# adaLN weights of a two-layer trunk in uncut 2 MB units with a buffer of their own

## The chip, the cores and the metric

The kernel runs on one core of one Trainium2 chip. The metric is device time in microseconds of one execution, the median of several. A core has five engines with queues of their own: TensorE (PE), VectorE (DVE), ScalarE (ACT), GpSimd (POOL) and SyncE (SP), and DMA engines that they share; here SP issues the weight loads.

## The reference

One inference step of a trunk of two layers for 256 latent and 128 context tokens, width 1024, fp32. Every layer is modulated by adaLN: nine vectors of 1024 (shift, scale and gate, three times) come from a product of the SiLU of a conditioning vector with a weight matrix of 1024 x 9216. There are two conditioning vectors, one for latent tokens and one for context tokens, so the product has two rows, but it reads all 36 MB of each layer's matrix.

```python
def adaln(cvec, l, p):
    m = jax.nn.silu(cvec) @ p['w_ada'][l] + p['b_ada'][l]
    return m.reshape(cvec.shape[0], N_MOD, D_MODEL)

def trunk_layer(x, mod, l, p, pos, ctx):
    sh1, sc1, g1, sh2, sc2, g2, sh3, sc3, g3 = [mod[:, i, None, :] for i in range(N_MOD)]
    x = x + 0.5 * g1 * swiglu(modulate(rms_norm(x, nw[0]), sh1, sc1), ...)
    m, new_ctx = mixer(modulate(rms_norm(x, nw[1]), sh2, sc2), l, p, pos, ctx)
    x = x + g2 * m
    x = x + 0.5 * g3 * swiglu(modulate(rms_norm(x, nw[2]), sh3, sc3), ...)
```

The mixer has one input projection and three heads beside each other (differential attention, latent attention `mla`, and a two-way S5 scan), then one output projection. Shift and scale of a part are needed before it begins, its gate when its first output rows are added to x.

## The kernel before

Activations stay on the chip, transposed (128 partitions of features x 8 blocks x 384 tokens). The program is, per layer, ffn(l, 0), mixer(l), ffn(l, 1). Every big product is made of three matmuls on split operands (`mm3`, lines 238 to 241): ACT copies a weight tile into `whi`, VectorE or POOL subtracts to get `wlo` (`split`, line 249), each with two buffers. Weight tiles come through `load` (line 243): 1 MB, [128, 2048], three buffers under one tag `raw`, issued on SP in program order. An up block of an ffn is 48 matmuls of a tile, a down block 36 or 30. The first 2048 adaLN columns of layer 0 are done ahead of everything with loads of their own (`start`, lines 1412 to 1426); all others are the subject here.

The remaining adaLN columns are cut into groups (`ada_steps`, line 278). Groups 0, 1 and 3 of a layer have 2048 columns, in 8 units of one k row (128 of the 1024 rows of the matrix); the other groups have 1024 columns, in 4 units of two k rows. A unit is one 1 MB `load` from the common ring and four matmuls per k row (line 293): the stationary operand is `conds`, 32 columns with two in use, and each of the four matmuls writes a quarter of the partitions of one PSUM bank, `adaps`, so that a k row of a group is four matmuls of 512 or 256 columns. In fp32 a matmul shows as two records in the profile: a k row has 8. At a group's end ACT copies the bank (`ad`), TensorE transposes it (line 301) and VectorE adds the bias in four instructions.

The units are steps in a list, `fillers`; the stages pop them at fixed places. An ffn pops one step after each up and each down block (`fill_after`), the mixer one after each of the products 3, 4 and 5 of its input projection, the rest spread evenly over 36 attention steps, and the last beside the output projection. Before, ffn(0, 0) has 12 units, mixer 0 has 32, both middle ffns have 2 each, and mixer 1 has 16. The steps of the preparation of the S5 tables (`prep`) sit in the same list in both ffns ahead of a mixer. One of them, `kext`, writes a table to DRAM (`kd`, line 752) and reads it back as 2048 pieces of 512 B (`Wi`, line 756), both on POOL's queue. A scheduler then places instructions on every engine; a matmul may be placed among others than those it is written beside. PE runs its own list strictly in order, and so does SP.

Of the kernel before, what the change touches and what calls it, by code (L numbers as in the profile page):

```python
# [20 lines left out]
DEPTH = 2  # L21
# [44 lines left out]
def _layout(inp):  # L66
    a = {k: np.asarray(v) for k, v in inp.items()}
    d = {}
# [3 lines left out]
    wa = w[:, :, :8192].reshape(2, 8, 128, 4, 2048).transpose(0, 3, 1, 2, 4).reshape(2, 32, 128, 2048)  # L72
    wb = w[:, :, 8192:].reshape(2, 4, 2, 128, 1024).transpose(0, 1, 3, 2, 4).reshape(2, 4, 128, 2048)
    d['wada'] = np.concatenate([wa, wb], 1)
    for z in range(2):
        wc = w[:, :, 4096 + 1024 * z:5120 + 1024 * z].reshape(2, 4, 2, 128, 1024).transpose(0, 1, 3, 2, 4)
        d['wada'][:, 16 + 4 * z:20 + 4 * z] = wc.reshape(2, 4, 128, 2048)
    d['wada'][0, :8] = w[0, :, :2048].reshape(8, 128, 2, 8, 128).transpose(3, 1, 0, 2, 4).reshape(8, 128, 2048)
# [98 lines left out]
def trunk(ctx, tc, I, O):  # L177
# [8 lines left out]
    def bank(name):  # L186
        return psp.tile([128, 512], F32, tag="P", name=name)
# [5 lines left out]
    def SMV(n):  # L193
        return sm[:, SM[n][0]:SM[n][1]]
# [38 lines left out]
    def act(out, a, f, **k):  # L233
        S.activation(out, a, f, **k)  # L234
# [40 lines left out]
    adaT = [cst.tile([128, 72, 2], F32, name=f"adaT{l}") for l in range(DEPTH)]  # L275
    bada = SMV('b_ada').rearrange("p (l b) -> p l b", l=2)

    def ada_steps(l, g):
        w = 512 if g in (0, 1, 3) else 256
        units = w // 64  # L280
        row = int(8 * g)
        st = {}

        def unit(u):
            raw = load(I['wada'][l, row + u])
            if u == 0:
                st['ps'] = psp.tile([128, 512], F32, tag="ada", name="adaps", bufs=1)
            ps = st['ps']
# [6 lines left out]
            if u == units - 1:  # L295
                ad = sp.tile([128, 512], F32, tag="ad", name="ad")
                act(ad[:, :w], ps[:, :w], AF.Copy)
                pt = bank("adapt")
                nch = w // 128
                for c in range(nch):  # L300
                    T.transpose(pt[:, c * 128:(c + 1) * 128], ad[:, c * 128:(c + 1) * 128], ident)
                b0 = 2 * row
                pv = pt[:, 0:nch * 128].rearrange("p (c q x) -> p q c x", c=nch, q=4)[:, :, :, 0:2]
                ov = adaT[l][:, b0:b0 + 4 * nch, :].rearrange("p (q c) x -> p q c x", c=nch)
                bv = bada[:, l, b0:b0 + 4 * nch].rearrange("p (q c) -> p q c", c=nch)
                for q in range(4):
                    add(ov[:, q], pv[:, q], bv[:, q, :, None].broadcast_to([128, nch, 2]))

        return [lambda u=u: unit(u) for u in range(units)]
# [336 lines left out]
    def s5_prep(l, s5p):  # L646
# [85 lines left out]
        def kext():  # L732
# [19 lines left out]
            nc.gpsimd.dma_start(kd.rearrange("c h g n -> g c h n"), kx.rearrange("p h j c -> p h (j c)"))  # L752
# [3 lines left out]
            nc.gpsimd.dma_start(wi.rearrange("p h g n -> p (h g) n"), win)  # L756
            P['Wi'] = wi

# [35 lines left out]
        steps += [lambda d=d, hf=hf: gtab(d, hf) for d in range(2) for hf in range(4)]  # L794
# [603 lines left out]
    def start(stp):  # L1398
# [4 lines left out]
        bv = bada[:, 0, 0:16].rearrange("p (z k) -> p z k", z=2)  # L1403
        pss = [[bank("up"), bank("up")] for _ in range(NF)]
        nx = 0
        for k in range(NB):
# [4 lines left out]
            raw = stp.tile([128, 2048], F32, tag="araw", name="araw", bufs=4)  # L1411
            nc.sync.dma_start(raw, I['wada'][0, k])
# [50 lines left out]
    N1, N2 = 16, 18  # L1463
    
    for l in range(DEPTH):
# [48 lines left out]
_NAMES = ('xT', 'wada', 'wfi', 'wfo', 'win', 'wout', 'wsm', 's5', 'small', 'lam', 'kc', 'vc', 'ckvc', 'kpec', 'const')  # L1514
# [14 lines left out]
```

## Time and profile before

| what | us |
|---|---|
| median of 3 runs | 1699.22 (1698.43 to 1699.89) |
| profiled execution, its own time | 1697.89 |
| its span | 1695.6 |
| PE busy | 1640.5 (97%) |
| VectorE busy | 1098.6 (65%) |
| ACT busy | 689.2 (41%) |
| POOL busy | 157.3 (9%) |
| mean granted clock of TensorE | 0.99 of full speed |

The span is the time between the first and the last instruction of the profiled execution. Busy time is an average over stages that differ, so the stages are read by themselves below: ffn(0, 0) from 46.0 us to 338.1, the products of mixer 0's input projection to 411.5, its attention and output projection to 586.4, ffn(0, 1) and ffn(1, 0) to 1163.1, the same two parts of mixer 1 to 1236.5 and 1399.7, and ffn(1, 1) to the end. A duration in the trace is that of one instruction or of a run of alike ones; consecutive matmuls overlap, so that the distance of two starts is less than the duration of one.

### The profile page before, as it was taken

The numbers are of one execution on the slowest core, as the hardware profiler recorded it, in microseconds if no ns is written. First come the engines' busy times: TensorE is split into PE (matmuls) and PEld (weight loads), VectorE is DVE, ScalarE is ACT, GpSimd is POOL, SyncE is SP. The second block draws the span as 40 slices with busy tenths as digits, with TensorE's granted clock in tenths as the row PEclk, the third lists the DMA queues.
The fourth block names the chain that finished last, engine by engine and source line by source line (L and its number), as shares of the span: only waits on it lengthen the run. The fifth ranks groups of instructions, "written<-read, shape, count | busy, mean of one in ns | idle before, by whom it ended". The sixth has DMA issues, their size and how long they took to land.

```text
span 1695.6 us, 26141 instructions
## 1 busy us (share of the span) xinstructions
PE 1640.5 (97%) x10144; PEld 1494.0 (88%) x10144; DVE 1098.6 (65%) x2752; ACT 689.2 (41%) x1295; POOL 157.3 (9%) x220
## 2 busy tenths in 40 slices
PE   7999999999999999999999999999998899999997
PEld 6888999998555899999999999999974589999997
DVE  6974576757465887577666555557745766555555
ACT  4332333533454533343344333335235654333333
POOL 1210110023001400000000000001301040000000
PEclk9999999999999999999999999999998999999999
DMA  9554542444576443354353333435436033333432
GB/s 377 198 214 163 140 151 97 157 162 144 191 270 237 139 171 118 125 124 137 93 180 137 118 136 109 141 95 172 148 128 226 26 103 122 125 124 112 139 101 84
DMA packets 45931, 251.47 MB, mean 148 GB/s; under 512 B 5600, under 2 KB 10576, under 8 KB 23920
## 3 DMA queue, kind: packets, MB, share of 16 engines
q1 hardware_dynamic: 41360, 241.12, 41.3%
q0 software_dynamic: 2144, 4.54, 1.1%
q10 hardware_dynamic: 2304, 4.15, 0.8%
q8 instruction: 79, 1.29, 0.3%
q14 instruction: 44, 0.36, 0.1%
HBM read 246.73 MB, written 3.05 MB: 147 GB/s over the span
## 4 chain that ended last, share of the span: by engine, by line
PE 88%; DVE 6%; ACT 3%; issue 1%; DMA 1%; POOL 0%; SPq 0%; DVEq 0%; ACTq 0%; POOLq 0%
PE up L239 15%; PE up L241 14%; PE up L240 14%; PE down L239 7%; PE down L241 7%; PE down L240 7%; PE adaps L293 4%; PE pj L239 2%; PE pj L241 2%; PE pj L240 2%; PE pout L241 1%; PE pout L239 1%; PE pout L240 1%; PE sc L1210 1%; PE po L1172 1%
## 5 line engine op out<-in xcount | busy, mean ns | idle before, releaser
L234 ACT ACTIVATE whi<-raw 128x1024 fp32r<-128x1024 f32 (+3 forms) x360 | 332.5, 925 | 660.0 <-PE up L240 337.1
L239 PE MATMUL up<-hh,whi 128*128 128x386 f32 x1408 | 474.4, 342 | 7.7 <-ACT whi L234 4.0
L241 PE MATMUL up<-hh,wlo 128*128 128x386 f32 x1408 | 478.3, 340 | 0.5 <-DVE wlo L213 0.5
L240 PE MATMUL up<-hl,whi 128*128 128x386 f32 x1408 | 478.3, 340 | 0.0
L213 DVE TENSOR_TENSOR wlo<-raw,whi 128x1024 fp32r<-128x1024 f32 (+2 forms) x318 | 347.5, 1093 | 49.0 <-ACT whi L234 46.2
L239 PEld LDWEIGHTS up<-hh,whi 128*128 128x128 f32 x1408 | 266.2, 190 | 15.5 <-ACT whi L234 5.3
L241 PEld LDWEIGHTS up<-hh,wlo 128*128 128x128 f32 x1408 | 265.6, 189 | 9.0 <-DVE wlo L213 2.2
L240 PEld LDWEIGHTS up<-hl,whi 128*128 128x128 f32 x1408 | 266.1, 189 | 1.5 <-issue 1.1
L241 PE MATMUL down<-hidh,wlo 128*128 128x384 f32 x704 | 236.3, 336 | 0.0
L239 PE MATMUL down<-hidh,whi 128*128 128x384 f32 x704 | 235.8, 335 | 0.0
L240 PE MATMUL down<-hidl,whi 128*128 128x384 f32 x704 | 235.3, 334 | 0.0
L231 DVE SCALAR_TENSOR_TENSOR xTt<-down,gate,xTt 128x256 f32<-128x256 f32 (+1 forms) x256 | 95.0, 413 | 115.0 <-PE down L241 115.0
L466 DVE COPY bb<-up 128x2 f32<-128x2 f32 x176 | 27.6, 158 | 190.3 <-PE up L241 189.8
L241 PEld LDWEIGHTS down<-hidh,wlo 128*128 128x128 f32 x704 | 132.1, 188 | 1.1 <-issue 0.6
L239 PEld LDWEIGHTS down<-hidh,whi 128*128 128x128 f32 x704 | 132.2, 188 | 1.0 <-ACT whi L234 0.8
L240 PEld LDWEIGHTS down<-hidl,whi 128*128 128x128 f32 x704 | 132.2, 188 | 0.0
L213 DVE TENSOR_TENSOR t<-up,R 128x384 f32<-128x384 f32 x176 | 95.5, 548 | 3.3 <-ACT R L234 3.2
L293 PE MATMUL adaps<-raw,conds 128*32 128x256 f32 (+1 forms) x704 | 85.3, 505 | 1.2 <-DMA raw<-in_wada 1.2
L239 PE MATMUL pj<-hh,whi 128*128 128x386 f32 (+1 forms) x240 | 84.3, 353 | 0.9 <-ACT whi L234 0.7
L234 ACT ACTIVATE hidh<-sl 128x384 fp32r<-128x384 f32 x88 | 46.1, 524 | 91.1 <-DVE sl L231 91.1
L241 PE MATMUL pj<-hh,wlo 128*128 128x386 f32 (+1 forms) x240 | 83.0, 347 | 0.0
L240 PE MATMUL pj<-hl,whi 128*128 128x386 f32 (+1 forms) x240 | 82.7, 346 | 0.0
(268 smaller groups left out, 1955.6 us busy)
## 6 DMA issues: line engine op xcount, KB each, us to landing
raw<-in_wfi SPq DMA_DIRECT2D x85, 1024.0 KB, 4.9
raw<-in_wada SPq DMA_DIRECT2D x64, 1024.0 KB, 5.1
raw<-in_wfo SPq DMA_DIRECT2D x32, 768.0 KB, 4.3
raw<-in_wfo SPq DMA_DIRECT2D x32, 640.0 KB, 4.0
raw<-in_win SPq DMA_DIRECT2D x14, 1024.0 KB, 4.8
araw<-in_wada SPq DMA_DIRECT2D x8, 1024.0 KB, 9.8
raw<-in_wout SPq DMA_DIRECT2D x16, 512.0 KB, 3.4
wr<-in_wfi SPq DMA_DIRECT2D x8, 384.0 KB, 9.7
```

The source lines that it names most:

```text
L213: return (eng or V).tensor_tensor(out, a, b, op=op)
L231: return V.scalar_tensor_tensor(out, a, s, b, op0=op0, op1=op1)
L234: S.activation(out, a, f, **k)
L239: T.matmul(out, whi, xhi, start=first, stop=False)
L240: T.matmul(out, whi, xlo, start=False, stop=False)
L241: marks.append(T.matmul(out, wlo, xhi, start=False, stop=last).ins)
L293: T.matmul(ps[32 * q:32 * q + 32, 0:w], conds[:, k, :], raw[:, c0:c0 + w], start=(k == 0), stop=(k == 7))
L466: V.tensor_copy(bb[:, z], ps[z][:, NT:NT + 2])
L1172: T.matmul(po[64 * h2:64 * h2 + 64, 0:256], vt[:, kt, 128 * b + 64 * h2:128 * b + 64 * h2 + 64], wTs[h2][:, kt, :], start=(kt == 0), stop= ...
L1210: T.matmul(sc, qT[p, self.b, t * 128:(t + 1) * 128], kT[p, self.b, self.k0:self.k0 + n], start=True, stop=True)
```

## The change

The columns of both layers behind the first 2048 are laid side by side and cut into eight groups of 2048 columns, each of 4 units of two k rows: a unit is one 2 MB load and eight matmuls of 512 columns. The units have a buffer of their own (`araw`, 16 KB per partition, one buffer) instead of the ring's. A unit's step is followed in the list by a step that issues the next unit's load, placed on SP behind the latest ring load written before it. A unit's matmuls may not be scheduled ahead of the latest `mm3` written before them (`issue_after(marks[-1])`). Groups 0 and 1 go to ffn(0, 0), groups 2 and 3 to mixer 0, group 4 to ffn(0, 1), group 5 to ffn(1, 0), groups 6 and 7 to mixer 1; in ffn(0, 0) the S5 preparation starts after the first eight steps. `kd` and `Wi` are issued on ACT's queue, `Wi` in a later step of the list than `kd` (at `gtab(0, 3)`). The scratch for descriptors of POOL's DMAs is set to 1024.

```diff
     def load(src, n=2048):
...
-            nc.sync.dma_start(raw[:, :n], src)
+            cur['load'] = nc.sync.dma_start(raw[:, :n], src).ins
...
-    def ada_steps(l, g):
-        w = 512 if g in (0, 1, 3) else 256
-        units = w // 64
-        row = int(8 * g)
+    pairs = [(g, u) for g in range(8) for u in range(4)]
+    ahead = []
+
+    def ada_load():
+        if pairs:
+            g, u = pairs.pop(0)
+            raw = wp.tile([128, 2, 4, 512], F32, tag="araw", name="araw", bufs=1)
+            with tc.issue_after(cur['load']):
+                nc.sync.dma_start(raw.rearrange("p k q n -> p (k q n)"), I['wada'][g, u])
+            ahead.append((g, u, raw))
+
+    def ada_steps(g):
...
-            raw = load(I['wada'][l, row + u])
+            if not ahead:
+                ada_load()
+            g_, u_, raw = ahead.pop(0)
...
-            for kk in range(8 // units):
-                k = u * (8 // units) + kk
-                for q in range(4):
-                    c0 = kk * 1024 + q * w
-                    T.matmul(ps[32 * q:32 * q + 32, 0:w], conds[:, k, :], raw[:, c0:c0 + w],
-                             start=(k == 0), stop=(k == 7))
+            with tc.issue_after(marks[-1]):
+                for kk in range(2):
+                    for q in range(4):
+                        T.matmul(ps[32 * q:32 * q + 32], conds[:, 2 * u + kk, :], raw[:, kk, q],
+                                 start=(u == 0 and kk == 0), stop=(u == 3 and kk == 1))
...
-        return [lambda u=u: unit(u) for u in range(units)]
+        out = []
+        for u in range(4):
+            out += [lambda u=u: unit(u), ada_load]
+        return out
...
-            nc.gpsimd.dma_start(kd.rearrange("c h g n -> g c h n"), kx.rearrange("p h j c -> p h (j c)"))
+            nc.scalar.dma_start(kd.rearrange("c h g n -> g c h n"), kx.rearrange("p h j c -> p h (j c)"))
...
-            nc.gpsimd.dma_start(wi.rearrange("p h g n -> p (h g) n"), win)
+            work['win'] = win
...
+        def kwin():
+            nc.scalar.dma_start(P['Wi'].rearrange("p h g n -> p (h g) n"), work['win'])
...
-    SKIP = 0
-    g1 = ada_steps(0, 1)
-    fillers += g1[:SKIP] + [both(f, g) for f, g in zip(g1[SKIP:], prep)] + inter(ada_steps(0, 2), prep[8 - SKIP:])
+    ada = [ada_steps(g) for g in range(8)]
+    w = ada[0] + ada[1]
+    fillers += w[:8] + [both(f, g) for f, g in zip(w[8:], prep)] + prep[8:]
...
-            fillers += a1[N2:]
+            fillers += ada[5]
...
-            fillers += ada_steps(0, 2.5) + ada_steps(0, 3) + ada_steps(0, 4)
-            a1 = ada_steps(1, 0) + ada_steps(1, 1) + ada_steps(1, 2)
-            fillers += a1[:N1]
+            fillers += ada[2] + ada[3]
         else:
-            fillers += ada_steps(1, 2.5) + ada_steps(1, 3) + ada_steps(1, 4)
+            fillers += ada[6] + ada[7]
...
-            mid = a1[N1:N2]
+            mid = ada[4]
...
-    nc = bacc.Bacc("TRN2", target_bir_lowering=False, num_devices=1)
+    nc = bacc.Bacc("TRN2", target_bir_lowering=False, num_devices=1, dynamic_dma_scratch_size=1024)
```

The order of the instructions of PE, first in ffn(0, 0), among the matmuls of an up block. Before:

```order
L241 MATMUL up<-hh_107,wlo 128x386
L293 MATMUL adaps<-raw,conds 32x512
L239 MATMUL up<-hh_100,whi 128x386
L240 MATMUL up<-hl_108,whi 128x386
L293 MATMUL adaps<-raw,conds 32x512 x3
L241 MATMUL up<-hh_100,wlo 128x386
L239 MATMUL up<-hh_101,whi 128x386
```

With the change:

```order
L236 MATMUL up<-hl_114,whi 128x386
L237 MATMUL up<-hh_106,wlo 128x386
L300 MATMUL adaps<-araw,conds 32x512 x8
L235 MATMUL up<-hh_99,whi 128x386
L236 MATMUL up<-hl_107,whi 128x386
L237 MATMUL up<-hh_99,wlo 128x386
```

A k row of 512 columns was cut by the scheduler into one and three matmuls with products between them; the eight matmuls of a unit now stand in one piece.

The order of PE in the attention of mixer 0, where `pq` are the query products of the latent attention, `qt2p` transposes of their result, `sc` scores and `wtp` transposes of weights. Before:

```order
L1280 MATMUL pq<-raw,cT 128x288 x2
L293 MATMUL adaps<-raw,conds 32x512 x4
L1280 MATMUL pq<-raw,cT 128x288 x2
L293 MATMUL adaps<-raw,conds 32x256 x8
L1289 MATMUL qt2p<-co,qt_4804 96x128 x6
L1280 MATMUL pq<-raw,cT 128x288 x4
L293 MATMUL adaps<-raw,conds 32x256 x8
L1289 MATMUL qt2p<-co,qt_4829 96x128 x6
L1210 MATMUL sc<-kT,qT 128x384 x4
```

With the change:

```order
L300 MATMUL adaps<-araw,conds 32x512 x8
L1292 MATMUL pq<-raw,cT 128x288 x4
L1301 MATMUL qt2p<-co,qt_4759 96x128 x6
L1292 MATMUL pq<-raw,cT 128x288 x4
L300 MATMUL adaps<-araw,conds 32x512 x8
L1301 MATMUL qt2p<-co,qt_4784 96x128 x6
L1222 MATMUL sc<-kT,qT 128x384 x4
L1177 MATMUL wtp<-co,e 128x128 x4
L1292 MATMUL pq<-raw,cT 128x288 x4
```

Pieces of four or eight matmuls stood between nearly all of these; now two whole units stand here, with two `pq` blocks and one `qt2p` between them, and the second is the first unit of a group.

The order of SP from the last tiles of mixer 0's input projection (`win`) to the output projection (`wout`); `wsm` is a small weight. Before:

```order
L246 DMA raw<-in_win 128x768
L246 DMA raw<-in_wada 128x2048 x3
L246 DMA raw<-in_wsm 128x1152
L246 DMA raw<-in_wada 128x2048 x16
L246 DMA raw<-in_wout 128x1024
L246 DMA raw<-in_wada 128x2048 x5
L246 DMA raw<-in_wout 128x1024
L246 DMA raw<-in_wada 128x2048 x4
L246 DMA raw<-in_wout 128x1024 x6
```

With the change:

```order
L242 DMA raw<-in_win 128x768
L242 DMA raw<-in_wsm 128x1152
L283 DMA araw<-in_wada 128x4096
L242 DMA raw<-in_wout 128x1024 x3
L283 DMA araw<-in_wada 128x4096 x3
L242 DMA raw<-in_wout 128x1024
L283 DMA araw<-in_wada 128x4096 x2
L242 DMA raw<-in_wout 128x1024
L283 DMA araw<-in_wada 128x4096
L242 DMA raw<-in_wout 128x1024 x3
```

The 1 MB loads of `wada` shared the ring `raw` with `wout`; the 2 MB loads of `araw` each follow the unit before in their one buffer, and `wout` loads stand behind them in SP's list.

## Rows read from the trace of the kernel before

**Rows 1.** windows by stage: start:end, us, engines' busy us (xcount), PEclk, DMA share, GB/s

```profile
46.00:338.10 292.10, 291.59 (x1718) 271.18 (x1717) 204.29 (x493) 108.86 (x174) 35.40 (x53) 1.00 0.48 157
...
411.50:586.40 174.90, 168.75 (x1074) 109.19 (x1075) 103.23 (x344) 86.35 (x233) 29.43 (x37) 0.98 0.58 211
586.40:1163.10 576.70, 574.42 (x3354) 567.67 (x3353) 384.51 (x858) 226.27 (x355) 11.66 (x41) 1.00 0.40 132
...
1236.50:1399.70 163.20, 151.24 (x937) 107.33 (x938) 95.78 (x319) 85.48 (x231) 28.35 (x36) 0.94 0.34 120
```

**Rows 2.** windows: the last 12 us of mixer 1's products

```profile
1225.00:1237.00 12.00, 8.12 (x60) 7.10 (x60) 11.68 (x25) 5.38 (x13) 2.35 (x2) 1.00 0.51 184
```

**Rows 3.** waits of PE: releaser, us in total, times, longest

```profile
PE vtp L882 <- ACT pjt L234: 7.8, 2, 3.9
...
PE qt2p L1289 <- DVE qt L213: 5.5, 4, 3.3
```

**Rows 4.** windows by stage, tile adaps alone

```profile
46.00:338.10 292.10, 18.76 (x128) 3.82 (x128) 0.00 (x0) 0.98 (x2) 1.00 0.48 157
338.10:411.50 73.40, 4.89 (x64) 1.78 (x64) 0.00 (x0) 0.00 (x0) 1.00 0.42 147
411.50:586.40 174.90, 35.88 (x256) 7.09 (x256) 0.00 (x0) 2.54 (x5) 0.98 0.58 211
586.40:1163.10 576.70, 4.89 (x64) 1.78 (x64) 0.00 (x0) 0.39 (x1) 1.00 0.40 132
...
1236.50:1399.70 163.20, 15.95 (x128) 3.67 (x128) 0.00 (x0) 1.36 (x3) 0.94 0.34 120
```

**Rows 5.** groups by line on PE: busy us, mean ns | idle before

```profile
L293 PE MATMUL adaps<-raw,conds 128*32 128x256 f32 (+1 forms) x704 | 85.3, 505 | 1.2 <-DMA raw<-in_wada 1.2
...
L301 PE MATMUL adapt<-co,ad 128*128 128x128 f32 x32 | 5.6, 285 | 0.5 <-ACT ad L234 0.5
```

**Rows 6.** timeline of PE: a 512-column k row in ffn(0,0), start us, duration us

```profile
99.39 0.34 PE L239 MATMUL up<-hh,whi 128*128 128x386 f32 x1
99.57 0.34 PE L240 MATMUL up<-hl,whi 128*128 128x386 f32 x1
99.84 1.06 PE L293 MATMUL adaps<-raw,conds 128*32 128x512 f32 x8
...
101.11 0.34 PE L239 MATMUL up<-hh,whi 128*128 128x386 f32 x1
```

**Rows 7.** timeline of PE: other adaLN pieces, in both ffns and mixer 1

```profile
118.84 1.04 PE L293 MATMUL adaps<-raw,conds 128*32 128x512 f32 x2
...
617.09 1.07 PE L293 MATMUL adaps<-raw,conds 128*32 128x256 f32 x16
...
884.12 0.63 PE L293 MATMUL adaps<-raw,conds 128*32 128x256 f32 x6
...
1253.27 1.92 PE L293 MATMUL adaps<-raw,conds 128*32 128x512 f32 x16
```

**Rows 8.** DMA issues: KB each, median us from issue to landing

```profile
raw<-in_wada SPq DMA_DIRECT2D x64, 1024.0 KB, 5.1
...
raw<-in_wout SPq DMA_DIRECT2D x16, 512.0 KB, 3.4
...
Wi<-kd POOLq DMA_DIRECT2D x2, 1024.0 KB, 22.7
...
kd<-kx POOLq DMA_DIRECT2D x2, 240.0 KB, 4.6
```

**Rows 9.** timeline of PE: attention of mixer 1 [idle before <- releaser]

```profile
1285.82 2.18 PE L1280 MATMUL pq<-raw,cT 128*128 128x288 f32 x8
...
1289.71 0.83 PE L1289 MATMUL qt2p<-co,qt 128*96 128x128 f32 x6 [0.72 <-DVE qt L213]
1290.38 2.11 PE L1280 MATMUL pq<-raw,cT 128*128 128x288 f32 x8
```

**Rows 10.** timeline of ACT in ffn(0,0) [idle before <- releaser]

```profile
279.78 1.06 ACT L234 ACTIVATE whi<-raw 128x1024 fp32r<-128x1024 f32 x1 [3.19 <-PE up L240]
```

More of the change, by code (lines that the diff above doesn't have):

```diff
@@ L71, in _layout @@
     w = a['w_ada']
[L72 to L78, printed above, removed]
+    d['wada0'] = w[0, :, :2048].reshape(8, 128, 2, 8, 128).transpose(3, 1, 0, 2, 4).reshape(8, 128, 2048)
+    w = np.concatenate([w[0, :, 2048:], w[1]], 1)
+    d['wada'] = w.reshape(4, 2, 128, 8, 2048).transpose(3, 0, 2, 1, 4).reshape(8, 4, 128, 4096)
     d['wfi'] = a['ffn_w_in'].reshape(2, 2, 8, 128, 2, NJ, 128).transpose(0, 1, 5, 3, 2, 4, 6).reshape(2, 2, NJ, 128, 2048)
@@ L274, in trunk @@
     act(conds[:, :, 0:2], SMV('cond').rearrange("p (k c) -> p k c", c=2), AF.Silu)
-    adaT = [cst.tile([128, 72, 2], F32, name=f"adaT{l}") for l in range(DEPTH)]
-    bada = SMV('b_ada').rearrange("p (l b) -> p l b", l=2)
-    def ada_steps(l, g):
-        w = 512 if g in (0, 1, 3) else 256
-        units = w // 64
-        row = int(8 * g)
+    adaA = cst.tile([128, 144, 2], F32, name="adaA")
+    adaT = [adaA[:, 72 * l:72 * l + 72] for l in range(DEPTH)]
+    bada = SMV('b_ada')
+    pairs = [(g, u) for g in range(8) for u in range(4)]
[8 more added lines that the diff above has]
+    def ada_steps(g):
         st = {}
         def unit(u):
-            raw = load(I['wada'][l, row + u])
+            if not ahead:
+                ada_load()
+            g_, u_, raw = ahead.pop(0)
+            assert (g, u) == (g_, u_)
             if u == 0:
@@ L288, in unit @@
             ps = st['ps']
-            for kk in range(8 // units):
-                k = u * (8 // units) + kk
-                for q in range(4):
-                    c0 = kk * 1024 + q * w
-                    T.matmul(ps[32 * q:32 * q + 32, 0:w], conds[:, k, :], raw[:, c0:c0 + w],
-                             start=(k == 0), stop=(k == 7))
[L295 to L305, printed above, removed]
-                for q in range(4):
-                    add(ov[:, q], pv[:, q], bv[:, q, :, None].broadcast_to([128, nch, 2]))
-        return [lambda u=u: unit(u) for u in range(units)]
+            with tc.issue_after(marks[-1]):
[3 more added lines that the diff above has]
+                                 start=(u == 0 and kk == 0), stop=(u == 3 and kk == 1))
+            if u == 3:
+                ad = sp.tile([128, 512], F32, tag="ad", name="ad")
+                act(ad, ps, AF.Copy)
+                pt = bank("adapt")
+                for c in range(4):
+                    T.transpose(pt[:, c * 128:(c + 1) * 128], ad[:, c * 128:(c + 1) * 128], ident)
+                b0 = 16 + 16 * g
+                pv = pt.rearrange("p (c q x) -> p q c x", c=4, q=4)[:, :, :, 0:2]
+                ov = adaA[:, b0:b0 + 16, :].rearrange("p (q c) x -> p q c x", c=4)
+                bv = bada[:, b0:b0 + 16].rearrange("p (q c) -> p q c", c=4)
+                for q in range(4):
+                    add(ov[:, q], pv[:, q], bv[:, q, :, None].broadcast_to([128, 4, 2]))
+        out = []
+        for u in range(4):
+            out += [lambda u=u: unit(u), ada_load]
+        return out
     def mods(l, i):
@@ L793, in s5_prep @@
         steps += [kext]
-        steps += [lambda d=d, hf=hf: gtab(d, hf) for d in range(2) for hf in range(4)]
+        steps += [lambda d=d, hf=hf: (gtab(d, hf), kwin() if (d, hf) == (0, 3) else None) for d in range(2) for hf in range(4)]
         steps += [etab]
@@ L1402, in start @@
         av = adaT[0][:, 0:16, :].rearrange("p (z k) x -> p z k x", z=2)
-        bv = bada[:, 0, 0:16].rearrange("p (z k) -> p z k", z=2)
+        bv = bada[:, 0:16].rearrange("p (z k) -> p z k", z=2)
         pss = [[bank("up"), bank("up")] for _ in range(NF)]
@@ L1410, in start @@
                 nx += 1
-            raw = stp.tile([128, 2048], F32, tag="araw", name="araw", bufs=4)
-            nc.sync.dma_start(raw, I['wada'][0, k])
+            raw = stp.tile([128, 2048], F32, tag="araw0", name="araw0", bufs=4)
+            nc.sync.dma_start(raw, I['wada0'][k])
             wr = stp.tile([128, NF, 256], F32, tag="wr", name="wr", bufs=4)
@@ L1511, in trunk @@
         (nc.sync if i % 2 else nc.scalar).dma_start(yv[:, a:b], xT[:, a:b])
-_NAMES = ('xT', 'wada', 'wfi', 'wfo', 'win', 'wout', 'wsm', 's5', 'small', 'lam', 'kc', 'vc', 'ckvc', 'kpec', 'const')
+_NAMES = ('xT', 'wada0', 'wada', 'wfi', 'wfo', 'win', 'wout', 'wsm', 's5', 'small', 'lam', 'kc', 'vc', 'ckvc', 'kpec', 'const')
 def kernel(**inputs):
```

1 line of the change is left out of this document (removed).

## The prediction

> **What bounds the kernel now.** The windows by stage come first [rows 1]: in the feed-forward stages, ffn(0,0) from 46.0 us and both middle ones from 586.4 us, TensorE is busy 291.59 of 292.10 us and 574.42 of 576.70 us. An instruction added there lengthens the kernel by what it costs TensorE, and one removed shortens it. The mixers differ. Their product part (338.1 to 411.5 us in layer 0) ends on VectorE: in its last 12 us VectorE is busy 11.68 and TensorE 8.12 [rows 2], and TensorE waits for `vtp` 3.9 us in each mixer [rows 3]. Their attention part has both idle time and a clock that is sometimes at its lower level: TensorE is busy 168.75 of 174.90 us at clock 0.98 in mixer 0, and 151.24 of 163.20 us at 0.94 in mixer 1 [rows 1]. The same windows for tile `adaps` alone [rows 4] say who holds the adaLN matmuls: 18.76 us in ffn(0,0), 35.88 in the attention of mixer 0, 15.95 in that of mixer 1, 4.89 in the product part of layer 0, 4.89 in both middle feed-forward stages together. These matmuls are 85.3 us in all, with a DMA wait of 1.2 us in the whole program [rows 5]. A measurement of this kernel can tell about 0.2% (3.4 us) from no change.
>
> **Price of a run.** A run of adaLN matmuls stands between products whose pitch is 99.57 - 99.39 = 0.18 us. Around a run of one 512-column k row the next-but-one product starts 101.11 - 99.57 = 1.54 us after the last one before it, where without the run it would be 0.36; the run costs 1.18, that is 0.12 more than its own 1.06 [rows 6]. With the same 0.12: two rows of 256 cost 1.07 + 0.12 = 1.19, a piece of up to three matmuls of 256 0.63 + 0.12 = 0.75, and two rows of 512 in one piece 1.92 + 0.12 = 2.04 [rows 7]. A piece of one matmul of 512 takes 1.04 [rows 7], as much as four. So the new unit (2.04) replaces two units of 512 (2.36) or two k rows in four units of 256 (2.38) at 0.32 less, if it stays whole.
>
> **Feed-forward stages, on the path.**
> - ffn(0,0): by the order, before has ten pieces of 512 (two units are cut 1 + 3), eight small and three large pieces of 256: 10 x 1.18 + 8 x 0.75 + 3 x 1.19 = 21.4. After has eight whole runs, 8 x 2.04 = 16.3. **-5.1**.
> - ffn(0,1): two pairs of 256 (2.4) become four runs (8.2); a group's four transposes now end here, 5.6 / 8 = 0.7 [rows 5]. **+6.5**.
> - ffn(1,0): two pairs and one small piece (3.1), with a short group end of about 0.4, become 8.2 + 0.7. **+5.4**.
> Sum **+6.8**. The 2 MB loads there have two steps, over 12 us, between units. A 1 MB load takes 5.1 us and a 512 KB load 3.4 [rows 8]; by that slope 2 MB takes 5.1 + 2 x 1.7 = 8.5 (bounds: 5.1, no growth, and 10.2, in proportion). No wait there.
>
> **Product parts.** Before, three pieces per mixer stand among the products. After, one run is ahead of the rotations of the last product, the other behind the products in the `vtp` wait. Ahead of VectorE's chain 1.92 takes the place of about 1.0; the second run hides in the 3.9 us wait [rows 3], if that cover goes it costs 2. **+0.95 each, +1.9.**
>
> **Attention parts.** The order puts u2 and u3 of the first group and four units of the second there, six units in either mixer. Six whole units are 6 x 1.92 = 11.5; the order cuts four of them into ten pieces, six more than whole, at about 0.8 each (1.04 less the piece's share of its run): 16.4 busy. Mixer 0 held 35.88, mixer 1 15.95 [rows 4]. What is 19.9 us more adaLN work made mixer 0 only 11.7 us longer (174.90 - 163.20): the rest filled idle time and kept the clock up (idle 6.2 against 12.0; clock loss 0.02 x 174.9 = 3.5 against 0.06 x 163.2 = 9.8). With 16.4 each, both should sit near mixer 1: 164.5 us. Mixer 0 **-10.4** (between -19.5, all of its busy time, and -5, half of that saving), mixer 1 **+1.3** (between -4 and +6, by the waits below).
>
> **The new wait.** With one buffer a load starts when TensorE has finished the unit before it. SP holds `wout` tiles behind those loads, so a late unit makes them late too. Between u3 and the first unit of the second group the order leaves only two `pq` blocks and one `qt2p`: 2.18 + 0.72 + 0.83 + 2.11 = 5.8, less overlap and plus the pass to SP and its issue about 6.5 us [rows 9]. Against the estimated 8.5 that is 2 us of waiting in each mixer, between 0 and 3.7; the neighbouring gaps are 9 to 10 us, so 0 to 1. Part of it lies where `qt2p` waits anyway, up to 3.3 us [rows 3], and the 1.2 us on a ring tile and the late `wout` go; so I leave it inside the 164.5. The Trainium skill (DMA: Bandwidth & Descriptors, Anatomy of one DMA) puts a transfer on the software queue at about 2.0 us plus its bytes over 436 GB/s. By it 2 MB would take 6.8 and the wait would be 0.3, a gain of under 2 us per mixer on my figure; its 4.4 for 1 MB is below the 5.1 of [rows 8], so the rows' slope stands.
>
> **kd and Wi on ACT.** They leave POOL's queue (a landing of 22.7 us for `Wi`, which includes the wait for `kd`) [rows 8]; nothing on the path waited there. On ACT, `Wi` waits for the landing of `kd`, 4.6 us at most, and behind it stand one `whi` and the feed-forward's activations. ACT has idled 3.19 us ahead of a `whi` in that stage [rows 10], and `whi` is double buffered. I take 0; bounds 0 and 4 for both layers. VectorE loses 12 small additions, off the path; the scratch size holds nothing that waits. Nothing.
>
> **Sum.** 6.8 + 1.9 - 10.4 + 1.3 + 0 = **-0.4 us** on the profiled execution's 1697.89, 1697.5; the median shown is 1.33 higher, so 1698.8.
>
> **The rivals.**
> - **B, slower: the single buffer.** In each attention the unit waits for its load at two or three places, the `wout` behind it on SP comes late, and the stretch after runs at the lower clock (1.2 GHz). Price: 2 x 2 + 2 us of waits per mixer and a clock of 0.94 or below in mixer 0 as well, 0.04 x 164 = 6.6: +7 to +16, 1706 to 1715. It decides once the landing passes 8 us. For: mixer 0, which has least idle time, has the clock at 0.98; mixer 1 at 0.94. Against: SP had no trouble serving 16 more MB in mixer 0. The Trainium skill (TensorE: Matmul & The Clock Gate, HAM oscillation) says that DMA waits between short bursts bring the clock down again and again; that speaks against this change, and in the traces mixer 1's lower clock beside its longer idle time agrees.
> - **C, faster: the waits go.** Weights get the ring alone, `wout` and `pq` are always early, and mixer 1's idle 12.0 us falls to mixer 0's 6.2 with a clock near 0.98: 6 + 6 in mixer 1, half of it in mixer 0 against my 164.5: -8 to -18, 1681 to 1691. For: in mixer 0 SP drew units through the same three tiles as the weights, without idle time. Against: the idle time is mostly that of `qt2p` on VectorE and `vtp` on ACT [rows 3], which the change doesn't touch.
> - **D, it doesn't save: cut runs.** If the scheduled order or the pitch makes two rows of 512 cost 2.36, the sixteen feed-forward runs add 16 x 0.32 = 5.1: 1704. [Rows 7] measured the 1.92 only between S5 operations; that is why it has a chance.
>
> **How the numbers follow.** The forecast has 0.5; its terms' bounds (mixer 0 by 5, mixer 1 by 4, the ACT wait up to 4) give it 1690 to 1706, and three parts in ten of it lie below -3.4, two above +3.4. B has 0.16, C 0.24, D 0.10 (in six of ten of its cases over +3.4). Faster: 0.5 x 0.3 + 0.24 = 0.39. Same: 0.5 x 0.5 + 0.04 = 0.29. Slower: 0.5 x 0.2 + 0.16 + 0.06 = 0.32. The range leaves out the outer half of C and the outer half of B: **1686 to 1710**.
>
> **What would show it.** `adaps` in the profile after: 512 columns alone, 256 x 2 records, about 70 us busy where 85.3 was; runs of x16 records with 1.9 us among the products. By stage: ffn(0,0) 287, the two middle ones 589, product parts 74.4, attention 164.5 each. The wait list has `adaps` on the DMA of `araw` with some 2 us in each attention; more than 6 in all, or a clock of 0.9 there, is rival B. Attention parts of 155 us or less are C. A feed-forward run over 2.2 us between products is D. ACT ahead of the `whi` behind `Wi` idle for over 5 us, with TensorE waiting on `whi`, would make the 0 for the moved DMAs wrong.

## The result and the profile after

The changed kernel takes 1709.93 us (median of 12 runs, 1703.03 to 1725.18) against 1698.99 (12 runs, 1694.60 to 1701.28): a ratio of 1.0071, 95% interval 1.0045 to 1.0098. It is slower by 0.7%, where 1698.8 was forecast and 1710 was the upper end of the range. The profiled execution took 1703.6 us, near the fastest of its kernel (span 1701.8, 6.2 more than before), so half of the loss doesn't show in its trace. The times of the kernel go with the mean granted clock of TensorE in the execution: 1703 us where that is 0.992, 1725 where it is 0.977. The trace of before has 0.990, that of after 0.992. At an equal clock the kernels are some 9 us apart: at 0.992 three executions of before, from all runs, took 1694.4 to 1694.6 us and three of the changed kernel 1703.0 to 1703.6; at 0.991 they took 1695.0 to 1697.4 and 1704.3 to 1705.9. The other 2 us of the 10.9 go with a lower clock, at the median 0.989 before and 0.987 after.

Windows by stage of the changed kernel (start:end, us, then busy us of PE, PEld, DVE, ACT and POOL with their counts, the granted clock, DMA share, GB/s). They answer to [rows 1, 4]:

```profile
338.50:413.10 74.60, 68.02 (x506) 62.44 (x505) 52.24 (x122) 24.22 (x44) 23.05 (x15) 1.00 0.39 137
413.10:577.20 164.10, 151.72 (x906) 105.61 (x905) 98.78 (x328) 86.67 (x233) 30.11 (x37) 0.97 0.35 126
577.20:1168.00 590.80, 586.66 (x3425) 569.90 (x3424) 385.60 (x864) 226.97 (x356) 8.85 (x39) 1.00 0.45 150
...
1242.70:1405.00 162.30, 149.37 (x906) 104.44 (x905) 93.08 (x313) 86.38 (x232) 28.26 (x36) 0.98 0.31 110
1405.00:1701.80 296.80, 283.64 (x1615) 281.82 (x1614) 173.40 (x357) 112.72 (x172) 1.41 (x6) 0.98 0.34 115
```

The same for tile `adaps` alone:

```profile
413.10:577.20 164.10, 17.58 (x96) 3.20 (x96) 0.00 (x0) 1.19 (x2) 0.97 0.35 126
577.20:1168.00 590.80, 15.39 (x128) 3.34 (x128) 0.00 (x0) 1.19 (x2) 1.00 0.45 150
...
1242.70:1405.00 162.30, 17.94 (x96) 3.27 (x96) 0.00 (x0) 1.19 (x2) 0.98 0.31 110
```

The stages against before, from the first product of each part to that of the next, in us (the boundaries of before taken the same way):

| stage | before | after | change | forecast |
|---|---|---|---|---|
| to the end of ffn(0,0) | 338.3 | 338.5 | +0.2 | -5.1 |
| products, mixer 0 and mixer 1 | 73.6 + 73.5 | 74.6 + 74.6 | +2.2 | +1.9 |
| attention, mixer 0 | 174.5 | 164.1 | -10.4 | -10.4 |
| ffn(0,1) and ffn(1,0) | 576.9 | 590.8 | +13.9 | +11.9 |
| attention, mixer 1 | 163.0 | 162.3 | -0.6 | +1.3 |
| ffn(1,1) to the end | 295.9 | 296.8 | +0.9 | 0 |

The attention parts came near the forecast in this execution, at clocks of 0.97 and 0.98. Both feed-forward terms are off, and waits that were not there before are a part of that. PE's waits by releaser (us in total, times, longest us), of after:

```profile
PE up L235 <- ACT hh L230: 4.4, 7, 1.5
...
PE adapt L307 <- ACT ad L230: 2.9, 4, 0.7
...
PE adaps L300 <- DMA araw<-in_wada: 2.3, 2, 1.2
...
PE up L237 <- DVE wlo L209: 1.7, 3, 1.2
...
PE up L235 <- ACT R L230: 0.6, 1, 0.6
```

The group of all units (busy us, mean ns | idle before) and the issue of its loads (KB, us to landing), of after; they answer to [rows 5, 8]:

```profile
L300 PE MATMUL adaps<-araw,conds 128*32 128x512 f32 x512 | 74.0, 613 | 2.3 <-DMA araw<-in_wada 2.3
```

```profile
araw<-in_wada SPq DMA_DIRECT2D x32, 2048.0 KB, 7.6
```

A 2 MB load landed in 7.6 us, below the 8.5 that the rows' slope gave. It was waited for twice, 2.3 us in all. The estimate of 6.8 by the fit of the Trainium skill (DMA: Bandwidth & Descriptors, Anatomy of one DMA), which is for the software queue, is 0.8 too low for these loads on SP's queue. One run in a down block, timeline of PE of after:

```profile
158.41 0.33 PE L236 MATMUL down<-hidl,whi 128*128 128x384 f32 x1
158.58 0.34 PE L237 MATMUL down<-hidh,wlo 128*128 128x384 f32 x1
158.85 1.92 PE L300 MATMUL adaps<-araw,conds 128*32 128x512 f32 x16
160.71 0.44 PE L235 MATMUL down<-hidh,whi 128*128 128x384 f32 x1
160.99 0.34 PE L236 MATMUL down<-hidl,whi 128*128 128x384 f32 x1
```

The next-but-one product starts 160.99 - 158.58 = 2.41 us after the last one ahead of the run, 0.36 of it its own: 2.05, the forecast 2.04. Rival D is out.

### The profile page after: what moved, and what is told of

Same layout as the page of the kernel before. It is cut to its first block, busy times and chain, and to the rows that moved or that the text cites. A ratio compares the mean times of both kernels' runs of the same rounds, so it can differ in the third digit from the quotient of the medians.

```text
span 1701.8 us, 25684 instructions
## 1 busy us (share of the span) xinstructions
PE 1630.1 (96%) x9952; PEld 1488.9 (87%) x9952; DVE 1090.3 (64%) x2740; ACT 690.2 (41%) x1292; POOL 153.0 (9%) x216
## 4 chain that ended last, share of the span: by engine, by line
PE 86%; DVE 7%; ACT 3%; issue 2%; DMA 1%; POOL 0%; ACTq 0%; SPq 0%; DVEq 0%
PE up L235 14%; PE up L236 13%; PE up L237 13%; PE down L235 7%; PE down L237 7%; PE down L236 7%; PE adaps L300 4%; PE pj L235 2%; PE pj L237 2%; PE pj L236 2%; PE pout L237 1%; PE pout L235 1%; PE pout L236 1%; DVE wlo L209 1%; PE po L1184 1%
## 5 line engine op out<-in xcount | busy, mean ns | idle before, releaser
L209 POOL TENSOR_TENSOR wlo<-raw,whi 128x512 fp32r<-128x512 f32 (+1 forms) x42 | 66.1, 1575 | 165.2 <-ACT whi L230 125.6
```

Of the source, the lines that this page charges most:

```text
L209: return (eng or V).tensor_tensor(out, a, b, op=op)
```

## The experiments

### The changed kernel again

Twice more, unchanged.

> The changed kernel once more, for a second trace and for the spread of its times. So far its times go with the mean granted clock: 1703.0 us at 0.992, 1725.2 at 0.977. Theory 1 (the clock falls in the attention parts): in an execution with a mean clock under 0.988 the attention parts of the two mixers show 0.90 to 0.94 where the first trace had 0.97 and 0.98, the feed-forward stages stay at 1.00, and all waits are as before. Theory 2 (the clock falls in the feed-forward stages, at the new waits of the transposes): the two mixers stay at 0.97 and a feed-forward stage is under 0.99. Theory 3 (transfers that take longer in some executions): the clock follows waits of adaps on the DMA of araw, which then exceed 6 us in all instead of 2.3.

> The changed kernel a third time, for one more trace and more times. Mean clock 0.977 to 0.992, times 1703 to 1725. Theory 1: whatever is lost over 1703 is lost in the two attention parts (under 0.95 there), with waits as in the first trace and the feed-forward stages at 1.00.

Medians 1711.60 (6 runs, ratio 1.0076, 1.0046 to 1.0106) and 1713.27 (5 runs, 1.0093, 1.0058 to 1.0128), mean clocks 0.977 to 0.991. The trace of the first shows where the clock goes; windows of the two attention parts of after_again (span 1712.1):

```profile
413.78:577.41 163.63, 150.62 (x905) 104.89 (x905) 98.83 (x329) 86.67 (x233) 30.11 (x37) 0.98 0.35 126
1242.74:1415.04 172.30, 159.97 (x906) 110.38 (x905) 93.83 (x314) 87.11 (x233) 28.32 (x36) 0.91 0.30 105
```

Mixer 1 is 10 us longer than in the first trace, at 0.91 instead of 0.98, with the same idle time (12.3 and 12.9) and the same waits. Two rows of the same place, timeline of PE, first of after, then of after_again:

```profile
1341.70 0.88 PE L1262 MATMUL sc<-kTh,qT 96*128 96x384 f32 x2 [1.70 <-DVE nm L1167]
...
1345.12 1.29 PE L1184 MATMUL po<-wT,vt 128*64 128x256 f32 x9
```

```profile
1346.00 1.62 PE L1262 MATMUL sc<-kTh,qT 96*128 96x384 f32 x2 [1.70 <-DVE nm L1167]
...
1351.46 2.40 PE L1184 MATMUL po<-wT,vt 128*64 128x256 f32 x9
```

In both, TensorE waits 1.70 us for VectorE's `nm`; in the second it comes back at the lower of its two levels: `sc` takes 1.62 us instead of 0.88, and the run of `po` that took 1.29 takes 2.40. Theory 1 holds for the place: the clock falls in an attention part, not in the feed-forward stages, and not at waits for DMA (theory 3). Only one mixer fell below 0.97, where the theory had both. The trace of after_third (1704.6 us) is like the first; none was taken of an execution at 0.977.

### Buffers and transfers

half_bufs: two 8 KB buffers of one k row each; the edit is below, without the line of the matmuls, which reads `raw[kk][:, q]`. half_swap: the same with the matmuls in the other order of halves, which undoes the double buffering.

```diff
-            raw = wp.tile([128, 2, 4, 512], F32, tag="araw", name="araw", bufs=1)
+            raw = [wp.tile([128, 4, 512], F32, tag="araw", name="araw", bufs=2) for _ in range(2)]
...
-                nc.sync.dma_start(raw.rearrange("p k q n -> p (k q n)"), I['wada'][g, u])
+                for kk in range(2):
+                    nc.sync.dma_start(raw[kk].rearrange("p q n -> p (q n)"), I['wada'][g, u, :, 2048 * kk:2048 * kk + 2048])
```

> The same 16 KB as two buffers of 8 KB, one k row each, so that the first half of the next unit loads while TensorE is at the second. Rival B of the prediction (the single buffer is what costs): the DMA waits of adaps, 2.3 us, go to 0, the attention parts are 2 us or more shorter in sum, and the clock stays at 0.99 in all executions. Theory 1: at most 2.3 us less in an execution with the same clock, and the same spread.

> The two 8 KB buffers again, but the matmuls of a unit take the half that lands last first and release the half that is loaded next last: the 1 MB transfers stay, the double buffering and the separate k rows go, and all eight matmuls of a unit stand in one piece. If the two small transfers made half_bufs fast, this is at 1699 too. If it is the finer grain (k rows landing one by one, so that pieces of four stand at more places of the attention parts and keep TensorE going), this is at 1706 or more, with attention parts that are 3 us or more longer in sum than those of half_bufs (162.9 and 159.5 us).

half_bufs took 1699.13 (ratio 0.9992, 0.9981 to 1.0003), half_swap 1698.72 (1.0001, 0.9988 to 1.0013): the loss is gone in both, so neither double buffering nor finer pieces explain it, and the transfers seemed to. But the scheduler had placed the units differently: in mixer 0 the pieces of the changed kernel are 1, 7, 8, 8, 1, 1, 1, 5, 6, 2, 4, 4 matmuls, those of half_swap 1, 7, 8, 8, 8, 8, 4, 4. The waits of `adaps` for DMA that half_bufs was to take away stayed, 2.5 us in two. Theory 4, that the cut pieces cost, came from the pieces, and one run, uncut_swap, holds everything but the transfers and buffers (its order on TensorE is that of uncut_all, below):

> uncut_all with the loads of half_swap: two transfers of 1 MB per unit into two halves, in the same order of instructions on TensorE as uncut_all. If one 2 MB transfer or its single buffer costs by itself, this is 2 to 6 us below uncut_all (1693.9); if only places and pieces count, it is the same within 2.

1696.35 (ratio 0.9978, 0.9966 to 0.9989) against 0.9969 (0.9958 to 0.9980) for uncut_all with one buffer and 2 MB transfers: no difference that can be told. With whole units, eight in a mixer, the single buffer and its 2 MB transfers cost nothing that these runs can tell; rival B falls as to its cause.

### Cut pieces

The edit, where `recent` holds every TensorE matmul and transpose written so far; uncut_v1 applies it to two units of the second group of each mixer alone:

```diff
-            with tc.issue_after(marks[-1]):
+            with tc.issue_after(recent[-1]):
                 for kk in range(2):
```

> The changed kernel (one 2 MB buffer, one 2 MB transfer per unit) with one thing else: the second and third unit of the second group of a mixer may not be placed ahead of the TensorE instruction written before them. By the order they then stand in one piece each, where the changed kernel has 1 + 1 + 1 + 5 and 6 + 2 matmuls; the pieces of a mixer are those of half_swap. Theory 4 (the cut pieces cost: a piece of one matmul takes as long as one of four, four pieces more in each mixer): each attention part has 4 to 5 us less TensorE work at full clock, 1699 to 1702, and few executions over 1705. If the 2 MB transfers or the single buffer cost, it stays at 1706 or more, half_swap having had the same pieces with 1 MB transfers at 1698.7.

> The same constraint for every unit: by the order all 32 units stand in one piece of eight. Theory 4: two further pieces less in each mixer, so up to 2 us per mixer below uncut_v1, if the later place costs nothing: 1696 to 1701. If places matter more than pieces (a unit that waits for the instruction ahead of it leaves TensorE idle there), it is slower than uncut_v1 with longer idle time in the attention parts at equal TensorE work.

uncut_v1 took 1704.21 (ratio 1.0031, 1.0018 to 1.0043), above its expectation, uncut_all 1693.91 (0.9969, 0.9958 to 0.9980): 16.0 us under the changed kernel, and faster than before. What a cut costs is plain in a timeline of PE: one unit in the attention of mixer 0, of after:

```profile
480.64 1.04 PE L300 MATMUL adaps<-araw,conds 128*32 128x512 f32 x2
...
482.46 1.05 PE L300 MATMUL adaps<-araw,conds 128*32 128x512 f32 x2
...
484.56 1.05 PE L300 MATMUL adaps<-araw,conds 128*32 128x512 f32 x2
...
486.74 1.90 PE L300 MATMUL adaps<-araw,conds 128*32 128x512 f32 x10
```

Three pieces of one matmul (two records) take 1.04 or 1.05 each and the rest 1.90: 5.0 us for what is 1.92 in one piece. The same windows of uncut_all, for all instructions of both attention parts, and for `adaps` in mixer 0:

```profile
412.84:569.98 157.14, 143.68 (x906) 103.01 (x905) 103.01 (x328) 84.92 (x232) 30.27 (x37) 0.98 0.37 131
1235.41:1390.45 155.04, 142.41 (x905) 103.24 (x904) 94.41 (x313) 85.35 (x232) 28.27 (x36) 0.98 0.32 116
```

```profile
412.84:569.98 157.14, 11.54 (x96) 2.50 (x96) 0.00 (x0) 1.20 (x2) 0.98 0.37 131
```

The six units take 11.54 us (6 x 1.92) instead of 17.58 and 17.94, and the attention parts 157.1 and 155.0 instead of 164.1 and 162.3, at the same clock of 0.98 or 0.97. That is 14.2 us, of which the pieces' own time is 12.4.

The medians do not go with the pieces alone: uncut_v1 has the pieces of half_swap in both mixers, and is 5.5 us slower. In its order on TensorE one unit of each mixer and some matmuls of the attention stand elsewhere, and its clocks are 0.982 to 0.988, those of half_swap 0.985 to 0.992. At an equal clock the two agree: at 0.986 they took 1702.2 to 1703.9 and 1701.1 to 1703.2. So at an equal clock the pieces can be told: at 0.988 the changed kernel took 1709.0 to 1709.6, uncut_v1 1699.3 and 1699.9, uncut_all 1694.1 and 1694.7; at 0.992 the changed kernel 1703.0 to 1703.6, uncut_all 1690.5. That is 13 to 15 us from the changed kernel to uncut_all, near the pieces' own 12.4; the rest of the 16.0 is clock. The constraint also moves the units to later places, so piece and place are not fully apart.

swap_cut: the other way round, one unit of each mixer cut into steps of its own in half_swap.

```diff
+            if g in (3, 7) and u == 1:
+                out += [lambda u=u: unit(u)] + [lambda u=u, p=p: unit(u, p) for p in ((1, 2), (2, 3), (3, 8))] + [ada_load]
```

> The other way round: half_swap, whose units were whole there, with the second unit of the second group of a mixer cut into 1 + 1 + 1 + 5 by steps of its own; transfers and buffers unchanged. Theory 4: three pieces more of 1.0 us in each mixer, 2 to 6 us over half_swap, so 1701 to 1705, and a wider spread of the clock if it is the cuts that bring it down. If transfers were the cause, it stays at 1698.7 within 2.

1706.83 (ratio 1.0045, 1.0029 to 1.0060), 8 us over half_swap and more than expected; the spread was not wider (clocks 0.985 to 0.988, where half_swap has 0.985 to 0.992). Its steps also take places away from others, so the 8 us are not the cuts' alone: at a clock of 0.985 it took 1706.0 to 1707.4 and half_swap 1703.6, 2 to 4 us apart.

### The wait of the transposes

The transposes of a group move into the next step of the list. late_tr does that to the changed kernel, uncut_late to uncut_all.

```diff
                 act(ad, ps, AF.Copy)
-                pt = bank("adapt")
-                for c in range(4):
...
+                st['ad'] = ad
+
+        def close():
+            if 'ad' in st:
+                ad = st.pop('ad')
+                pt = bank("adapt")
+                with tc.issue_after(marks[-1]):
+                    for c in range(4):
...
-            out += [lambda u=u: unit(u), ada_load]
+            out += [lambda u=u: unit(u), lambda: (close(), ada_load())]
```

> A group's transposes stand one step of the list later, so that the ACT copy ahead of them has long ended. If the four waits of adapt on ACT (2.9 us in all) lie on the path of the feed-forward stages, they go, and an execution with the clock of the first trace (0.992) takes 1701 instead of 1703.6: ffn(0,0) is 1.4 us shorter, both middle stages together 1.4. If they only took the place of other waits: 1703.6. The spread of the clock stays (theory 1) or goes with these waits (theory 2: all executions at 0.99).

> uncut_all with a group's transposes one step later. The waits of adapt on ACT (2.9 us in four, two in ffn(0,0) and one in either middle stage) go from stages in which TensorE is busy all the time: 1.4 us less in the two middle stages, up to 1.4 in ffn(0,0), so 1691 to 1692.5. If other waits take their place: 1693.9.

late_tr took 1710.31 (ratio 1.0052, 1.0035 to 1.0068): its middle stages are 1.5 us shorter (589.3), ffn(0,0) ends 0.4 earlier although its start took 1.0 longer, and its attention parts were at 0.94 and 0.93 in the trace, 10 us longer together. So the wait is real, and the median, with its lower clock, couldn't show it; at a clock of 0.987 late_tr took 1705.0 and 1705.7 and the changed kernel 1710.7. uncut_late took 1685.51 (ratio 0.9916, 0.9905 to 0.9928), 8.4 us under uncut_all and 13.5 us under the kernel before. Waits of uncut_all:

```profile
PE adapt L185 <- ACT ad L243: 5.7, 8, 0.7
```

In uncut_late this row is gone. Windows of its attention of mixer 0, the middle stages and the attention of mixer 1:

```profile
411.98:567.31 155.33, 145.64 (x905) 104.76 (x904) 100.68 (x328) 85.46 (x232) 29.87 (x37) 0.96 0.37 132
567.31:1156.61 589.30, 586.59 (x3426) 569.90 (x3426) 385.60 (x864) 227.01 (x356) 8.90 (x39) 1.00 0.45 150
1231.21:1386.63 155.42, 145.39 (x905) 104.76 (x904) 93.60 (x313) 85.58 (x232) 28.49 (x36) 0.96 0.33 116
```

Idle time fell from 157.14 - 143.68 = 13.5 to 9.7 us in mixer 0, from 12.6 to 10.0 in mixer 1, and the middle stages by 1.5. That is more than the 2.9 expected, since in uncut_all all eight groups wait, two in each mixer among them. These waits are 5.7 us of the 8.4; where the rest comes from no run shows.

### Where the units stand

mix12 moves group 4 from ffn(0,1) into mixer 0; half_late_mix16 moves groups 4 and 5 there, on half_bufs with late transposes; best_last adds the constraint of uncut_all for all units, mix16_uncut1 only for those of mixer 1.

```diff
-            fillers += ada[2] + ada[3]
+            fillers += ada[2] + ada[3] + ada[4] + ada[5]
...
-            mid = ada[4]
+            mid = []
```

> Group 4 moves from ffn(0,1) into mixer 0, which then has 12 units, mixer 1 still 8. Theory 1 with the prediction's prices: ffn(0,1) loses four runs of 2.04, a group's transposes 0.7 and their wait 0.7, so 9.5 us; the attention of mixer 0 grows by 4 to 6 us (12 us for 20 us of adaLN work was the rate between the mixers before), and its clock is higher: 3 to 6 us less than the changed kernel in an execution of the same clock, 1698 to 1701, and a narrower spread. If the single buffer bounds mixer 0 (twelve loads of 7.6 us and the passes between them, in 100 us), mixer 0 grows by 10 or more with waits of adaps on DMA over 5 us.

> Two half buffers, transposes one step later, and groups 4 and 5 moved from the middle feed-forward stages into mixer 0, as many adaLN columns there as in the kernel before. By the prediction's prices the two middle stages lose 8 runs of 2.04 and two group ends of 1.4, 19 us; mixer 0 gains 8 units, 16 us busy, at the rate between the mixers before (0.6) some 10 us: 8 to 10 us less than half_bufs, 1689 to 1692, below both kernels. If the two half buffers bound mixer 0 (28 loads of 5.7 us, two in flight, against 100 us), its attention part is over 180 us, adaps waits on DMA more than 5 us, and the time is 1697 or more.

> half_late_mix16 with the constraint of uncut_all: groups 4 and 5 in mixer 0, two half buffers, transposes one step later, and no piece of fewer than three matmuls, where half_late_mix16 has four of one in mixer 0. Theory 4: 3 to 4 us below half_late_mix16 (1690.3), so 1686 to 1688; if the later place leaves idle time, 1690 or more.

> half_late_mix16 (1690.3) with the constraint of uncut_all for the units of mixer 1 alone, which then stand in pieces of 8, 8, 8, 8, 8, 4, 4, 8 (before 1 + 7 and 3 + 5 among them). Theory 4: two pieces less in mixer 1, about 2 us: 1687 to 1689. The attention part of mixer 1 at about 155 us instead of 157, all else the same.

mix12 took 1714.27 (4 runs, ratio 1.0083, 1.0068 to 1.0097), the second of its two cases: twelve units through one buffer. Its DMA waits, and its attention of mixer 0, 19 us longer than in after:

```profile
PE adaps L300 <- DMA araw<-in_wada: 9.8, 4, 7.6
```

```profile
413.10:596.20 183.10, 163.26 (x973) 107.87 (x972) 99.29 (x330) 87.46 (x233) 29.87 (x37) 0.95 0.44 158
```

half_late_mix16 took 1690.31 (0.9948, 0.9934 to 0.9961), the time that the prices gave: its middle stages were 572.0 us, 18.9 less than in half_bufs, mixer 0 174.4. best_last missed: 1703.19 (1.0026, 1.0015 to 1.0038), mixer 0 190.0 us with 19.2 us idle, and six waits of `adaps` for DMA, 15.2 us. That a unit kept behind the instruction ahead of it also releases its half later is the likely reason; no run tried it. mix16_uncut1 took 1686.41 (0.9922, 0.9908 to 0.9936). Its windows, in the order of uncut_late's:

```profile
410.72:585.30 174.58, 167.86 (x1042) 108.97 (x1042) 100.46 (x336) 87.80 (x235) 30.15 (x37) 0.97 0.61 213
585.30:1157.27 571.97, 569.26 (x3290) 566.12 (x3289) 384.84 (x857) 225.50 (x354) 8.86 (x39) 1.00 0.39 126
1231.87:1388.61 156.74, 147.31 (x906) 106.21 (x904) 93.73 (x313) 85.57 (x232) 28.44 (x36) 0.95 0.32 114
```

Its attention of mixer 1 is 156.7 us at a clock of 0.95, where 155 was expected. It and uncut_late beat both kernels, by two ways; best_last, which joins them on two half buffers, does not.

### Queue of kd and Wi, and idle time filled

b_kdact: the kernel before with `kd` and `Wi` issued on ACT as in the change, `Wi` at `gtab(0, 3)`. zero_fill adds this to the changed kernel in attention steps without a unit; its results stay the same, since the stationary operand is zero:

```diff
+                    if n == 0 and cur.get('open') is not None:
+                        cv = conds.rearrange("p k c -> p (k c)")
+                        for q in range(4):
+                            T.matmul(cur['open'][32 * q:32 * q + 32, 0:256], zer, cv, start=False, stop=False)
```

> The kernel before with kd and Wi alone moved to ACT's queue, Wi at the later step. The prediction took 0, bounds 0 to 4: 1698 to 1702, with ffn(0,0) and the middle stages as before within 1 us. Rival: ACT waits for the landing of kd with weight copies behind it, whi then ends later than TensorE wants it: up to 5 us in ffn(0,0) and as much in ffn(0,1).

> The changed kernel with useless matmuls in the attention steps that have no unit: a stationary operand of zeros, 256 columns of a resident tile, added into the open group (its sums stay the same), 76 in each mixer, 10 to 20 us of TensorE time there. Theory 1 (TensorE that is idle too often loses its clock there): the mean clock is 0.990 or more in all executions, no execution is over 1% above the fastest, and each attention part grows by less than half of the work that is added; the median may even fall below 1710. If the clock doesn't depend on this, both parts grow by what is added and the spread of the clocks (0.977 to 0.992) stays.

b_kdact took 1699.93 (ratio 1.0000, 0.9990 to 1.0009): the moved DMAs cost nothing that can be told. zero_fill took 1716.61 (5 runs, 1.0111, 1.0094 to 1.0129), clocks 0.987 to 0.991. No execution came near 0.977, but not all reached 0.990, and TensorE work in small pieces (8.7 and 10.9 us more on `adaps`) made the parts longer by 6.6 and 11.8 us than in the first trace, where theory 1 had less than half of what is added. That filling holds the clock up is neither shown nor excluded.

## Why the prediction was wrong

It forecast no change, -0.4 us by its sum; the kernel lost 10.9 us by the medians, 6.2 in the profiled execution's span, some 9 at an equal clock.

- **The price of a run** was right: 2.05 measured, 2.04 taken. All units together took 74.0 us, about 70 expected, from 85.3.
- **ffn(0,0), -5.1: failed, +0.2.** This is the step that failed most. It took "TensorE is busy 291.59 of 292.10 us" for the whole stage, so that a piece removed shortens it by its price. In the first third that doesn't hold: three k rows of the kernel before stood where, or shortly before, TensorE has to wait without them. Timeline of PE of before:

```profile
48.94 1.06 PE L293 MATMUL adaps<-raw,conds 128*32 128x512 f32 x8
...
50.72 1.29 PE L239 MATMUL up<-hh,whi 128*128 128x386 f32 x6
...
55.25 1.07 PE L293 MATMUL adaps<-raw,conds 128*32 128x512 f32 x8
56.25 0.45 PE L239 MATMUL up<-hh,whi 128*128 128x386 f32 x1
...
90.16 1.06 PE L293 MATMUL adaps<-raw,conds 128*32 128x512 f32 x8
```

The same places of after, without units:

```profile
49.93 0.83 PE L398 MATMUL pr<-ones,acc 128*128 128x1 f32 x6 [0.26 <-DVE adaA L209]
51.39 1.29 PE L235 MATMUL up<-hh,whi 128*128 128x386 f32 x6 [0.63 <-ACT hh L230]
...
56.57 0.44 PE L235 MATMUL up<-hh,whi 128*128 128x386 f32 x1 [0.58 <-ACT R L230]
...
96.74 0.44 PE L237 MATMUL up<-hh,wlo 128*128 128x386 f32 x1 [1.15 <-DVE wlo L209]
```

From the 100th to the 150th up matmul before takes 13.8 us with two k rows between them, after 13.5 with none: 0.3 gained for a price of 2.4. From the 300th to the 350th before takes 10.0 with one k row, after 10.3 with none. The traces of all runs with the change have these 13.5 and 10.2 to 10.3, but for one 14.8 in uncut_swap, where the clock was low; b_kdact has the 13.8 and 10.0 of before. The last of the four waits lies where VectorE, which makes `wlo`, is busy without a gap, before and after:

```profile
80.00:100.00 20.00, 20.00 (x116) 17.55 (x120) 20.00 (x40) 6.25 (x10) 10.17 (x10) 1.00 0.57 211
```

```profile
80.00:100.00 20.00, 18.78 (x109) 16.44 (x108) 20.00 (x41) 6.78 (x10) 8.20 (x10) 1.00 0.55 211
```

By 97.4 us before has done 350 up matmuls, after needs 98.8 for them, although it had 3.0 us less adaLN work up to there (before five k rows in six pieces of 1.18, after two runs of 2.04): 1.4 + 3.0 = 4.4 of the 5.3 us that are missing. Of these, 0.7 are there already at the 100th up matmul (43.4 and 44.1 us): that is the start, which differs between executions of the same program (44.8 in after_again). This is read from the traces; no run put a unit back there, and the change also begins the S5 preparation on VectorE at a later step, which may have a part in the wait for `wlo`. The rest, 0.9, lies behind that, where the transposes of two groups wait:

```profile
124.11 1.92 PE L300 MATMUL adaps<-araw,conds 128*32 128x512 f32 x16
126.75 0.66 PE L307 MATMUL adapt<-co,ad 128*128 128x128 f32 x4 [0.72 <-ACT ad L230]
127.16 0.43 PE L235 MATMUL up<-hh,whi 128*128 128x386 f32 x1
```

They now stand right behind the last unit of a group and wait 0.72 us for ACT's copy of the bank, four times in the feed-forward stages. The prediction has no term for this wait. From the 100th up matmul to the end of the stage after takes 294.4 us, late_tr 293.0: 1.4 less, the two waits of this stage.

- **Middle stages, +11.9: +13.9.** Again the transposes, 2 x 0.72, shown by late_tr and uncut_late (1.5 us less). The other 0.5, and the 0.9 of the last stage, are not explained.
- **Product parts, +1.9:** +2.2, as forecast.
- **Attention parts, 164.5 each:** 164.1 and 162.3 in the profiled execution. The 16.4 us for the cut units were 17.6 and 17.9. That mixer 1 came out so near is in part luck: the number was taken over from a mixer 1 at a clock of 0.94, and this execution had 0.98; at 0.91 mixer 1 took 172.3. The step counted on a clock loss of 9.8 us per mixer at the most; in after_again mixer 1 loses 0.09 x 172.3 = 15.5, and over all executions the mean clock reaches down to 0.977, where that of the kernel before stays within 0.985 to 0.992. The clock of one trace was taken for all executions; by the medians that is 2 us of the loss. And the step accepted the cuts as a fixed part of the order: the runs show 16 us for taking them out, 13 to 15 at an equal clock.
- **The new wait, up to 2 us in each mixer:** 2.3 us in all. Rival B's time came true (1706 to 1715), its clock in part, its cause not: with whole pieces one buffer and 2 MB transfers serve as well as halves (uncut_swap). Where the rows show the clock fall, TensorE had waited for VectorE, 1.70 us, and not for DMA. So the rule named there, on DMA waits between short bursts (the Trainium skill, TensorE: Matmul & The Clock Gate, HAM oscillation), isn't what the rows show.
- **kd and Wi, 0:** shown by b_kdact.
- **Rival C** had the wrong reason, but attention parts of 155 us exist: with whole units.

What stays open: why the changed kernel's clock varies from 0.977 to 0.992 between executions and that of uncut_all only from 0.987 to 0.993. Cut pieces go with it in the changed kernel, but swap_cut, with cuts, has no wider spread than half_swap, and uncut_v1 has a lower clock than half_swap with the same pieces.

## What to carry to other kernels

A large transfer "in one piece" says nothing about its matmuls: count the pieces in the scheduled order, since a piece of one quarter-array matmul costs as much as four, and hold a unit together by a constraint on the instruction written before it, if its loads can bear the later place (best_last lost 12.9 us by it). Work that a scheduler puts right behind its producer on another engine (the transposes behind ACT's copy) belongs one step later on a full engine. And split a stage before you call it bound by an engine: a small piece of work may stand in a wait, where its removal gains nothing.

## What was not expected of the hardware

A matmul with 32 output partitions alone takes 1.04 us and four of them to four quarters 1.06 [rows 6, 7], so that cutting four into 1 + 3 doubles their time: that was known from the rows, not that taking the cuts out would give more than the whole loss. One program was run at mean clocks between 0.977 and 0.992, with times of 1703 to 1725 us, while the kernel before took 1694 to 1703 in the runs beside it; the clock fell behind a wait of 1.70 us that was passed at full clock in another execution of the same program. Moving 2 MB took 7.6 us where 1 MB took 5.1 [rows 8].
